# Other constants, and a shared port, in the model that orders TensorE's work in a two-layer decoder trunk

## The chip, the core and the metric

The kernel runs on one core of a Trainium2 chip. A core has TensorE (PE: matrix multiplications into PSUM), VectorE (DVE), ScalarE (ACT), GpSimd (POOL) and SyncE (SP, which here only issues DMAs). Each engine works through its own queue in order, and semaphores make an instruction wait for one on another engine. The metric is the device time in microseconds; less is better.

## The reference

A sequence of 1024 tokens of width 1024 goes through two layers, in float32. The first layer has a combined projection that feeds sliding-window attention (8 query heads, 2 key heads, window 128, rotary positions, a learned sink per head) and four heads of a gated delta rule in chunks; both outputs are concatenated and projected. The second layer is a recurrent block: a gate branch, a causal convolution of width 4 and a linear recurrence over time. Behind each mixer, and behind each MLP, stands a layer norm of `alpha * x + y`:

```
for layer in range(DEPTH):
    mix = hybrid_mixer(x, ...) if layer % 2 == 0 else recurrent_mixer(x, ...)
    x = layer_norm(DN_ALPHA * x + mix, ln1_g[layer], ln1_b[layer])
    x = layer_norm(DN_ALPHA * x + sqrelu_mlp(x, mlp_w1[layer], mlp_w2[layer]), ln2_g[layer], ln2_b[layer])
```

The MLP is `relu(x @ w1) ** 2 @ w2` with 4096 hidden units.

## The kernel before

**Precision.** Large products are made of three fp32r matmuls: each operand is split into a high part (a cast to fp32r) and a low part (the rest), and `mm3` (line 359) adds high by high, high by low and low by high. Every block of weights (128 x 1024, tile `ws`) is therefore cast to `wh` on ScalarE, or every fifth one on VectorE, and subtracted into `wl` on VectorE, or in some stages every second one on GpSimd (`split` and `wblock`, lines 343 to 357). Activations are split in the same way. The small products inside attention and the delta rule are plain fp32 matmuls.

**Streams and mixers.** The sequence is cut in two halves of 512 tokens, and each half is a stream (`stream`, line 1332) that runs through hybrid layer, MLP, recurrent layer and MLP, as a Python generator that yields after every few matmuls. A second kind of generator, a mixer, holds a chain of small steps in which TensorE and the other engines take turns: attention of a block of 128 queries (`attn_prep`, `attn_block`), one head of the delta rule (`head_mid`, line 949), the transposes of a layer norm (`layernorm`, line 451). A mixer yields a function of time, as `at(...)` (line 219), before each step of TensorE that needs a result of another engine.

**The order.** The loop at line 1361 writes TensorE's order by hand. While tracing, an object of the class `Clock` (line 60) keeps a model of the engines: a list of placed operations for VectorE (V), ScalarE (S), GpSimd (G) and DMA (D), and `now`, the time at which TensorE would be free. If a mixer's step is ready 0.5 us before `now` (MARGIN, line 27), its TensorE instructions are emitted next, and otherwise a unit of a stream. Each TensorE instruction is tied to the one before it (`_pe`, line 196). So the model's times decide how many matmuls of the streams stand between two steps of a chain; a step that comes too early in that order makes TensorE wait, for everything behind it too.

In the model `issue` (line 141) takes the ends of the operations that wrote the inputs, adds a hop for the consuming engine (`HOP`), and `place` (line 114) finds the next free spot on the engine's list and pushes what stands behind it. A duration is a constant and a slope per element (`NS`). `ready` (line 111) adds TensorE's hop. A matmul is costed in `matmul` (line 203):

```
c = 0.00042 * n * (1 if rhs.dtype == F32R else 4) if lhsT.shape[-1] > 32 else 0.046
```

The model also picks which tile of a ring is used next (`touch`, line 77: the one last used longest ago) and when the DMAs of `w2_sums` (line 515) are issued, which add quarters of w2 in DRAM, one on SyncE's queue and one, accumulating, on GpSimd's. The order of VectorE, ScalarE and GpSimd is set elsewhere: a scheduler that sees the whole program orders them with costs of its own.

Of the kernel before, what the change touches and what calls it, by code (L numbers as in the profile page):

```python
# [10 lines left out]
F32R = mybir.dt.float32r  # L11
# [4 lines left out]
PSUM = bass.MemoryType.PSUM  # L16

P = 128
D = 1024
# [30 lines left out]
NOSYNC = mybir.DependencyInfo(mybir.DependencyClass.NoSync, mybir.DependencyReason.SCHED_ONLY)  # L50


class Op:
    __slots__ = ("key", "t", "c", "end", "lag", "users")

    def __init__(self, key, t, c, lag=0.0):
        self.key, self.t, self.c, self.end, self.lag, self.users = key, t, c, t + c + lag, lag, []


class Clock:  # L60

    HOP = dict(V=0.3, S=0.3, G=0.3, P=0.40, D=0.0)
    NS = dict(V=(0.07, 1.04e-3), S=(0.095, 0.83e-3), G=(0.073, 2.25e-3))

    def __init__(self, tc, nc):
        self.tc, self.pe, self.now, self.last = tc, nc.tensor, 0.0, None
# [47 lines left out]
    def place(self, op, t):  # L114
        q = self.queue[op.key]
        i = bisect.bisect_left(q, t, key=lambda x: x.t)
        if i and q[i - 1].t + q[i - 1].c > t:
            t = q[i - 1].t + q[i - 1].c
        while i < len(q) and q[i].t <= t:
            t = max(t, q[i].t + q[i].c)  # L120
            i += 1
        op.t, op.end = t, t + op.c + op.lag
        q.insert(i, op)
        e = t + op.c
        while i + 1 < len(q) and q[i + 1].t < e:
            self.push(q[i + 1], e)

    def push(self, op, t):
        if t > op.t and op in self.queue[op.key]:
            self.queue[op.key].remove(op)  # L130
            self.place(op, t)
            for u in op.users:
                self.push(u, op.end + self.HOP[u.key])

# [3 lines left out]
        for a in outs:  # L138
            self.written.setdefault(a.name, {})[self.span(a)] = op

    def issue(self, key, outs, ins, c, t=0.0, lag=0.0, fresh=True):
        src = list(self.hits((self.written,), ins))
        war = list(self.hits((self.read, self.written), outs)) if fresh else []
        t = max([t] + [o.end + self.HOP[key] for o in src] + [o.end for o in war])
        for a in outs:
            t = max(t, self.old.get(a.name, 0.0), self.first.get(self.tag.get(a.name), 0.0))
        op = Op(key, t, c, lag)
        if key != "P":
            q = self.queue[key]
            while len(q) > 600:  # L150
                q.pop(0)
            self.place(op, t)
            for o in src + war:
                o.users.append(op)
        for a in outs:
            if a.name in self.tag:
                self.first[self.tag.pop(a.name)] = self.old[a.name] = op.t
        self.note(op, outs, ins)
        if key == "P":
            self.held.add(outs[0].name)  # L160
        else:
            self.held.difference_update(a.name for a in ins)
        return op

    def engine(self, eng, key):
        clk = self

        class Engine:
            def __getattr__(self, op):
                f = getattr(eng, op)  # L170

                def call(*a, **k):
                    aps = [x for x in (*a, *k.values()) if isinstance(x, bass.AP)]
                    outs = aps[:1] + ([k["accum_out"]] if "accum_out" in k else [])
                    if op == "tensor_tensor_reduce":
                        outs.append(aps.pop())
                    ins = aps[1:]
                    r = f(*a, **k)  # L178
# [24 lines left out]
    def matmul(self, out, lhsT, rhs, start, stop, fresh=False):  # L203
        n = int(np.prod(rhs.shape[1:]))
        c = 0.00042 * n * (1 if rhs.dtype == F32R else 4) if lhsT.shape[-1] > 32 else 0.046
        ins = self.pe.matmul(out, lhsT, rhs, start=start, stop=stop, skip_group_check=fresh)  # L206
        return self._pe(ins, out, [lhsT, rhs], c, start or fresh)

    def transpose(self, out, x, ident):
        return self._pe(self.pe.transpose(out, x, ident), out, [x], 0.00042 * 2 * out.shape[-1])  # L210


@with_exitstack
# [1293 lines left out]
```

## Time and profile before

| | |
|---|---|
| Median of 3 runs | 2313.34 us (2312.12 to 2314.28) |
| Profiled execution | 2313.61 us, span of its instructions 2311.8 us |
| TensorE busy | 2226.8 us (96%), 12460 matmuls |
| VectorE busy | 1552.7 us (67%) |
| ScalarE busy | 1026.1 us (44%) |
| GpSimd busy | 313.6 us (14%) |
| Mean granted TensorE clock | 0.988 of full |

In the lines of the profile PE is TensorE's matmuls, PEld its weight loads, and L178 and L206 are the lines of the model's helpers through which nearly every instruction is issued, so groups are told apart by their tiles: `wh` and `wl` are split weights, `ws` weights as loaded, `g`, `t`, `s` and `f` rings of activations, `mm` and `mx` PSUM banks of streams and mixers, `asc` and `hsc` small scalars of attention and of the delta rule, `lnw` those of layer norms, `S` the state of the delta rule. `mx<-t` is an operation that reads `t` and writes `mx`. In a row of a group, "busy, mean ns | idle before" follow the count. In the timeline a row has its start, its duration, and in brackets how long its engine sat idle before it and what ended that. TensorE's busy time counts an operation to its modelled end, so short waits between pipelined matmuls do not show as idle.

### The profile page before, as it was taken

What the parts mean: (1) busy time and instruction counts of PE and PEld (TensorE: products, weight loads), DVE (VectorE), ACT (ScalarE), POOL (GpSimd) and SP (SyncE); (2) the same over time, 40 slices, a digit from 0 to 9 for tenths busy, and PEclk for the clock granted to TensorE, in tenths of its full rate; (3) what the DMA queues carried; (4) which work ended last, traced back from release to release, by engine and by line L of the source; (5) the groups of instructions that cost most, each with busy time, mean ns of one, the idle gap of its engine ahead of it and who ended that gap; (6) DMA issues with size and microseconds to landing.
All of it is one profiled execution on the core that took longest, in us unless ns stands there. A gap on an engine that the chain in (4) does not pass through costs nothing.

```text
span 2311.8 us, 32057 instructions
## 1 busy us (share of the span) xinstructions
PE 2226.8 (96%) x12460; PEld 1795.1 (78%) x12460; DVE 1552.7 (67%) x2706; ACT 1026.1 (44%) x1759; POOL 313.6 (14%) x248
## 2 busy tenths in 40 slices
PE   8999997999999999999999999989999999999997
PEld 7676776667777888788888878868888887888886
DVE  6788759456645463686666898675565566776477
ACT  5364424433433233454444677474424434444442
POOL 3433223223322120000000001021100000000100
PEclk9999998999999999999999999999999999999999
DMA  4221232556667656677744335222523443454341
GB/s 159 65 74 36 75 123 74 146 153 180 178 177 231 193 162 187 191 237 232 222 139 155 119 129 170 93 74 96 182 95 127 138 146 125 156 166 137 128 159 69
DMA packets 86200, 329.08 MB, mean 142 GB/s; under 512 B 9504, under 2 KB 9888, under 8 KB 77856
## 3 DMA queue, kind: packets, MB, share of 16 engines
q1 hardware_dynamic: 72944, 272.17, 34.4%
q0 software_dynamic: 4608, 33.56, 7.6%
q10 hardware_dynamic: 8496, 21.30, 2.7%
q8 instruction: 98, 1.61, 0.3%
q14 instruction: 54, 0.44, 0.1%
HBM read 318.60 MB, written 75.50 MB: 170 GB/s over the span
## 4 chain that ended last, share of the span: by engine, by line
PE 78%; DVE 13%; ACT 3%; issue 2%; POOL 0%; DMA 0%; DVEq 0%; ACTq 0%; POOLq 0%
PE mm L206 61%; PE mx L206 16%; DVE g L178 5%; DVE t L178 2%; DVE s L178 2%; DVE hsc L178 2%; DVE wl L178 1%; PE mx L210 1%; DVE f L178 1%; ACT wh L178 1%; ACT g L178 1%; ACT t L178 1%; ACT s L178 1%; ACT f L178 0%; ACT L178 0%
## 5 line engine op out<-in xcount | busy, mean ns | idle before, releaser
L206 PE MATMUL mm<-g,wh 128*128 128x512 f32 x2816 | 890.1, 397 | 2.7 <-DVE g L178 2.6
L178 DVE TENSOR_TENSOR wl<-ws,wh 128x1024 fp32r<-128x1024 f32 (+1 forms) x374 | 456.8, 1222 | 340.0 <-ACT wh L178 336.7
L178 ACT CAST wh<-ws 128x1024 fp32r<-128x1024 f32 (+1 forms) x350 | 365.1, 1043 | 719.9 <-PE mm L206 620.6
L206 PEld LDWEIGHTS mm<-g,wh 128*128 128x128 f32 x2816 | 522.2, 189 | 111.3 <-DVE g L178 3.9
L206 PE MATMUL mm<-g,wl 128*128 128x512 f32 x1408 | 551.8, 392 | 0.0
L206 PE MATMUL mm<-wh,s 128*128 128x512 f32 x1152 | 379.8, 395 | 3.6 <-DVE g L178 3.3
L206 PEld LDWEIGHTS mm<-g,wl 128*128 128x128 f32 x1408 | 266.0, 189 | 57.0
L178 POOL TENSOR_TENSOR wl<-ws,wh 128x1024 fp32r<-128x1024 f32 (+1 forms) x64 | 157.2, 2457 | 1010.1 <-ACT wh L178 861.4
L206 PEld LDWEIGHTS mm<-wh,s 128*128 128x128 f32 x1152 | 216.2, 188 | 51.1 <-DVE g L178 3.9
L206 PE MATMUL mm<-wh,g 128*128 128x512 f32 (+1 forms) x768 | 231.4, 379 | 9.3 <-ACT wh L178 6.4
L206 PE MATMUL mm<-wl,s 128*128 128x512 f32 x576 | 224.6, 390 | 0.0
L206 PE MATMUL mx<-wh,s 128*128 128x512 f32 x528 | 172.7, 392 | 1.8 <-DVE s L178 1.8
L206 PEld LDWEIGHTS mm<-wh,g 128*128 128x128 f32 x768 | 142.3, 190 | 35.9 <-ACT wh L178 6.4
L206 PE MATMUL mm<-wl,g 128*128 128x512 f32 (+1 forms) x384 | 143.8, 375 | 0.3 <-DVE wl L178 0.3
L178 ACT CAST s<-g 128x512 fp32r<-128x512 f32 x158 | 96.4, 623 | 100.3 <-PE mm L206 51.2
L178 DVE TENSOR_TENSOR s<-g,s 128x512 fp32r<-128x512 f32 x158 | 106.8, 687 | 38.7 <-ACT s L178 38.5
L206 PEld LDWEIGHTS mm<-wl,s 128*128 128x128 f32 x576 | 108.3, 188 | 20.6 <-DVE wl L178 0.3
L206 PEld LDWEIGHTS mx<-wh,s 128*128 128x128 f32 x528 | 99.1, 188 | 23.2 <-DVE s L178 3.1
L178 DVE CAST wh<-ws 128x1024 fp32r<-128x1024 f32 x88 | 62.7, 712 | 78.1 <-PE mm L206 68.4
L178 DVE TENSOR_TENSOR g<-g,mm 128x512 f32<-128x512 f32 x144 | 95.0, 683 | 20.0 <-PE mm L206 19.5
L206 PE MATMUL mx<-wl,s 128*128 128x512 f32 x264 | 102.8, 389 | 0.0
L206 PEld LDWEIGHTS mm<-wl,g 128*128 128x128 f32 x384 | 73.2, 191 | 12.2 <-DVE wl L178 0.6
(241 smaller groups left out, 2703.2 us busy)
## 6 DMA issues: line engine op xcount, KB each, us to landing
ws<-w SPq DMA_DIRECT2D x234, 512.0 KB, 3.3
ws<-t SPq DMA_DIRECT2D x88, 512.0 KB, 3.3
t<-w POOLq DMA_DIRECT2D x32, 1024.0 KB, 8.6
ws<-hin_fm SPq DMA_DIRECT2D x32, 512.0 KB, 3.3
t<-w SPq DMA_DIRECT2D x16, 1024.0 KB, 7.5
t<-t SPq DMA_DIRECT2D x16, 1024.0 KB, 6.5
ws<-rin SPq DMA_DIRECT2D x32, 512.0 KB, 3.3
ws<-hout SPq DMA_DIRECT2D x16, 512.0 KB, 3.3
```

The source lines that it names most:

```text
L178: r = f(*a, **k)
L206: ins = self.pe.matmul(out, lhsT, rhs, start=start, stop=stop, skip_group_check=fresh)
L210: return self._pe(self.pe.transpose(out, x, ident), out, [x], 0.00042 * 2 * out.shape[-1])
```

## The change

The edit lies in the model alone. The hop that a consumer adds shrinks (V and S 0.3 to 0.06, G 0.3 to 0.1, P 0.40 to 0.3), and each operation instead has a lag after its duration that also counts for whoever overwrites its operands (V 0.085, S 0.1, G 0.08, P 0.17). TensorE's `now` leaves the lag out, and a matmul no longer waits for an earlier matmul on the same bank. An fp32r matmul is costed at 0.443 ns a column instead of 0.42; an fp32 one at 0.04 us and 1.2 ns a column (2 ns where the output has 64 rows and n is over 128) instead of 1.68 ns a column; one with at most 32 output rows at 0.03 us instead of 0.046. A scan on VectorE has twice the slope, a `scalar_tensor_tensor` of 128 elements or more 0.05 us more. New is the port: all operations of G, and those of V named in `PORT` whose operands all lie in SBUF, exclude each other, both when an operation is placed (`shared`) and when one that is placed later pushes others back.

```
+PORT = {"tensor_tensor", "scalar_tensor_tensor", "tensor_scalar"}
...
-    HOP = dict(V=0.3, S=0.3, G=0.3, P=0.40, D=0.0)
-    NS = dict(V=(0.07, 1.04e-3), S=(0.095, 0.83e-3), G=(0.073, 2.25e-3))
+    HOP = dict(V=0.06, S=0.06, G=0.1, P=0.3, D=0.0)
+    NS = dict(V=(0.07, 1.04e-3), S=(0.1, 0.83e-3), G=(0.07, 2.27e-3))
+    LAG = dict(V=0.085, S=0.1, G=0.08, P=0.17)
...
+    def shared(self, key, t):
+        q = self.queue["G" if key == "V" else "V"]
+        i = bisect.bisect_right(q, t, key=lambda x: x.t)
+        return q[i - 1].t + q[i - 1].c if i and q[i - 1].port and q[i - 1].t + q[i - 1].c > t else t
+
+    def place(self, op, t):
+        q = self.queue[op.key]
+        while True:
+            i, t = self.gap(op.key, t)
+            u = self.shared(op.key, t) if op.port else t
+            if u <= t:
+                break
+            t = u
         op.t, op.end = t, t + op.c + op.lag
         q.insert(i, op)
         e = t + op.c
         while i + 1 < len(q) and q[i + 1].t < e:
             self.push(q[i + 1], e)
+        if op.port:
+            r = self.queue["G" if op.key == "V" else "V"]
+            for o in r[bisect.bisect_right(r, t, key=lambda x: x.t):][:20]:
+                if o.t >= e:
+                    break
+                if o.port:
+                    self.push(o, e)
...
-        war = list(self.hits((self.read, self.written), outs)) if fresh else []
+        war = [o for o in self.hits((self.read, self.written), outs) if key != "P" or o.key != "P"] if fresh else []
...
-                    if key == "V" and op == "tensor_copy" and ins[0].space != PSUM:
+                    sbuf = all(x.space != PSUM for x in ins + outs)
+                    if key == "V" and op == "tensor_copy" and sbuf:
                         c1 *= 0.5
-                    clk.issue(key, outs, ins, c0 + c1 * n)
+                    if op == "tensor_tensor_scan":
+                        c1 *= 2.0
+                    if op == "scalar_tensor_tensor" and n >= 128:
+                        c0 += 0.05
+                    port = key == "G" or (key == "V" and sbuf and op in PORT)
+                    clk.issue(key, outs, ins, c0 + c1 * n, 0.0, clk.LAG[key], True, port)
...
-        self.now = self.issue("P", [out], reads, cost, self.now, 0.0, fresh).end
+        o = self.issue("P", [out], reads, cost, self.now, self.LAG["P"], fresh)
+        self.now = o.t + o.c
...
-        c = 0.00042 * n * (1 if rhs.dtype == F32R else 4) if lhsT.shape[-1] > 32 else 0.046
+        if rhs.dtype == F32R:
+            c = 0.000443 * n
+        elif lhsT.shape[-1] <= 32:
+            c = 0.03
+        else:
+            c = 0.04 + (0.002 if n > 128 and lhsT.shape[-1] == 64 else 0.0012) * n
...
-        return self._pe(self.pe.transpose(out, x, ident), out, [x], 0.00042 * 2 * out.shape[-1])
+        return self._pe(self.pe.transpose(out, x, ident), out, [x], 0.00085 * out.shape[-1])
```

More of the change, by code (lines that the diff above doesn't have):

```diff
@@ L50, with __init__ @@
 NOSYNC = mybir.DependencyInfo(mybir.DependencyClass.NoSync, mybir.DependencyReason.SCHED_ONLY)
+PORT = {"tensor_tensor", "scalar_tensor_tensor", "tensor_scalar"}
 class Op:
-    __slots__ = ("key", "t", "c", "end", "lag", "users")
-    def __init__(self, key, t, c, lag=0.0):
+    __slots__ = ("key", "t", "c", "end", "lag", "users", "port")
+    def __init__(self, key, t, c, lag=0.0, port=False):
         self.key, self.t, self.c, self.end, self.lag, self.users = key, t, c, t + c + lag, lag, []
+        self.port = port
 class Clock:
-    HOP = dict(V=0.3, S=0.3, G=0.3, P=0.40, D=0.0)
-    NS = dict(V=(0.07, 1.04e-3), S=(0.095, 0.83e-3), G=(0.073, 2.25e-3))
+    HOP = dict(V=0.06, S=0.06, G=0.1, P=0.3, D=0.0)
+    NS = dict(V=(0.07, 1.04e-3), S=(0.1, 0.83e-3), G=(0.07, 2.27e-3))
+    LAG = dict(V=0.085, S=0.1, G=0.08, P=0.17)
     def __init__(self, tc, nc):
@@ L112, in ready, with gap @@
         return max((o.end for o in self.hits((self.written,), aps)), default=0.0) + self.HOP["P"]
-    def place(self, op, t):
-        q = self.queue[op.key]
+    def gap(self, key, t):
+        q = self.queue[key]
         i = bisect.bisect_left(q, t, key=lambda x: x.t)
@@ L121, in place @@
             i += 1
+        return i, t
+    def shared(self, key, t):
[10 more added lines that the diff above has]
+            t = u
         op.t, op.end = t, t + op.c + op.lag
@@ L139, in note, with issue @@
             self.written.setdefault(a.name, {})[self.span(a)] = op
-    def issue(self, key, outs, ins, c, t=0.0, lag=0.0, fresh=True):
+    def issue(self, key, outs, ins, c, t=0.0, lag=0.0, fresh=True, port=False):
         src = list(self.hits((self.written,), ins))
-        war = list(self.hits((self.read, self.written), outs)) if fresh else []
+        war = [o for o in self.hits((self.read, self.written), outs) if key != "P" or o.key != "P"] if fresh else []
         t = max([t] + [o.end + self.HOP[key] for o in src] + [o.end for o in war])
@@ L146, in issue @@
             t = max(t, self.old.get(a.name, 0.0), self.first.get(self.tag.get(a.name), 0.0))
-        op = Op(key, t, c, lag)
+        op = Op(key, t, c, lag, port)
         if key != "P":
```

## The prediction, made before the result was known

> **What bounds the kernel now.** I read the page's busy shares first, then one table of five stretches (core 0, busy time of PE, PEld, DVE, ACT, POOL in each, then the granted clock).
>
> ```profile
> span 2311.8 us, 32057 instructions
> PE 2226.8 (96%) x12460; PEld 1795.1 (78%) x12460; DVE 1552.7 (67%) x2706; ACT 1026.1 (44%) x1759; POOL 313.6 (14%) x248
> ...
> 17.00:751.40 734.40, 689.72 (x5608) 527.89 (x5607) 493.42 (x1161) 300.83 (x749) 220.82 (x172) 0.97 0.42 125
> 751.40:1502.80 751.40, 744.16 (x3333) 612.71 (x3332) 521.00 (x775) 361.81 (x510) 45.28 (x49) 1.00 0.54 171
> 1502.80:1530.00 27.20, 18.91 (x87) 14.70 (x86) 23.88 (x35) 21.59 (x34) 4.67 (x2) 0.81 0.18 59
> 1530.00:2254.20 724.20, 719.23 (x3182) 593.62 (x3181) 459.98 (x606) 320.09 (x437) 39.72 (x18) 1.00 0.41 136
> 2254.20:2311.80 57.60, 44.49 (x196) 36.18 (x194) 42.78 (x98) 12.79 (x17) 0.00 (x0) 0.92 0.19 68
> ```
>
> TensorE is the bound, and the change takes no work from it. Only its idle time can be won: 734.4 - 689.7 = 44.7 us in the first stretch (attention and delta rule between matmuls), 7.2, 8.3 and 5.0 in the next three. The last stretch's 13.1 is mostly the final layer norm, which nothing can fill. Then the stretches in which the granted clock is a half, up to 751 us and the one at 1510:
>
> ```profile
> 144.96:151.79 6.83, 6.02 (x20) 5.24 (x21) 5.77 (x25) 5.78 (x23) 0.74 (x1) 0.50 0.02 7
> 192.75:199.57 6.83, 6.05 (x46) 2.94 (x48) 5.68 (x14) 2.33 (x4) 1.28 (x1) 0.50 0.07 23
> 366.83:370.24 3.41, 3.41 (x11) 2.83 (x10) 3.41 (x10) 1.06 (x2) 0.00 (x0) 0.50 0.00 0
> 383.89:390.72 6.83, 3.03 (x38) 2.51 (x39) 6.83 (x16) 4.55 (x17) 1.60 (x3) 0.50 0.00 0
> 397.55:407.79 10.24, 8.21 (x51) 5.04 (x51) 7.14 (x14) 1.66 (x3) 4.29 (x3) 0.50 0.39 120
> 633.07:636.48 3.41, 3.41 (x26) 2.23 (x28) 1.31 (x2) 0.57 (x1) 0.00 (x0) 0.50 1.10 190
> 1510.29:1520.53 10.24, 5.77 (x14) 3.90 (x15) 9.63 (x15) 4.93 (x8) 4.02 (x2) 0.50 0.17 51
> ```
>
> The first six hold 30.1 us of PE work at half speed, so 15.1 us are lost there; the last loses 2.9. What a better order could win at most is 44.7 + 15.1 = 59.8 us in the first stretch, 8.3 + 2.9 = 11.2 around 1510, and 12.2 elsewhere. Whom PE waits for (total us, times, longest), from the view of waits:
>
> ```profile
> PE mx L206 <- DVE t L178: 16.3, 8, 7.0
> PE mx L210 <- DVE g L178: 15.2, 9, 5.7
> PE mm L206 <- DVE g L178: 9.6, 11, 2.2
> ...
> PE mx L206 <- DVE s L178: 6.3, 7, 2.6
> PE mx L206 <- DVE S L178: 5.3, 3, 3.0
> PE mx L206 <- DVE g L178: 3.9, 3, 2.2
> PE mx L206 <- ACT t L178: 3.2, 4, 1.2
> ```
>
> These 45 waits are for VectorE nearly always: a small group was put into TensorE's order before its operand was there. The longest, in the timeline (start, duration; POOL, then DVE, then PE):
>
> ```profile
> 375.43 1.34 POOL L178 TENSOR_TENSOR f<-f,t 128x512 f32<-128x512 f32 x1 [11.36 <-PE mx L210]
> 378.41 2.41 POOL L178 TENSOR_TENSOR wl<-ws,wh 128x1024 fp32r<-128x1024 f32 x1 [1.63 <-ACT wh L178]
> ...
> 375.65 5.71 DVE L178 TENSOR_TENSOR g<-g,s 128x512 f32<-128x512 f32 x4
> ...
> 381.89 1.15 DVE L178 SCALAR_TENSOR_TENSOR f<-f,sm,f 128x512 f32<-128x512 f32 x1
> ...
> 383.24 1.88 DVE L178 TENSOR_TENSOR g<-g,s 128x512 f32<-128x512 f32 x3
> ...
> 387.69 0.65 PE L206 MATMUL mx<-t 32*32 32x32 f32 x32 [7.00 <-DVE t L178]
> ```
>
> Three of those DVE operations take 1.88 us where nothing is beside them, four take 5.71 beside POOL: 5.71 - 4 x 0.63 = 3.2 us too long. The scalar_tensor_tensor's 1.15 also overlaps POOL work; against the 0.63 that is 0.5. So 3.7 of the 7.0 us are VectorE and GpSimd excluding each other. That this is general shows in the spread (min/median/max ns) of two groups of tiny or equal DVE operations:
>
> ```profile
> L178 DVE TENSOR_TENSOR g<-g,asc x24: 426/1174/2875, 122.9 to 499.4; 128x512 f32<-128x512 f32 x21, 128x256 f32<-128x256 f32 x3
> L178 DVE TENSOR_TENSOR hsc<-hsc x128: 149/164/2478, 45.9 to 780.1; 128x4 f32<-128x4 f32 x80, 128x8 f32<-128x8 f32 x48
> ```
>
> The longest of a four-element operation is 2.5 us, as long as one POOL split of weights (2.41 above).
>
> **The change, part by part.** No instruction is added or removed; places in TensorE's order move, and with them buffers (picked by the model's last use) and the program order of what feeds them. Its time is the same matmuls plus the idle above, so I price each part in idle.
>
> *Port.* The model now pushes a VectorE operation with all operands in SBUF behind a GpSimd one and the reverse, and what depends on it. A step that was issued too early then gets more matmuls ahead of it. By the 3.7 of 7.0 us I give the port half of the first stretch's loss: 29.9 us. How much is caught? None if the collisions fall elsewhere than in the model, 29.9 if all are foreseen. A split on POOL starts when ScalarE has cast its block, which the model times too, but VectorE's order is not written by this model. I take two thirds: -20 us. Around 1510 the wait began before POOL worked at all, so I take nothing there:
>
> ```profile
> 1505.88 0.60 PE L210 MATMUL mx<-csb,g 128*128 128x128 f32 x4
> ...
> 1509.64 4.08 POOL L178 TENSOR_TENSOR wl<-ws,wh 128x1024 fp32r<-128x1024 f32 x1 [18.84 <-DVE g L178]
> ...
> 1512.17 1.11 PE L210 MATMUL mx<-csb,g 128*128 128x128 f32 x4 [5.69 <-DVE g L178]
> ```
>
> *Rule on the same port.* In the first stretch 17 DVE casts of weights have a mean of 803 ns, while all 88 have 712:
>
> ```profile
> L178 DVE CAST wh<-ws 128x1024 fp32r<-128x1024 f32 (+1 forms) x17 | 13.7, 803 | 16.4 <-PE mm L206 16.4
> ...
> L178 DVE CAST wh<-ws 128x1024 fp32r<-128x1024 f32 x88 | 62.7, 712 | 78.1 <-PE mm L206 68.4
> ```
>
> The other 71 then have 690, so casts too are held up, by 17 x 113 ns = 1.9 us; the changed model leaves tensor_copy out of its set. The Trainium skill (SBUF — State Buffer, "Who interferes with whom") says the same against the change: copies and casts can take the shared pair as well, and whoever starts first keeps it for the whole instruction. By that the term would be some 2 us smaller; the trace agrees on the direction, with 1.9 us.
>
> *Shorter hops.* A PE-VectorE-PE step on 128x512 was counted 0.3 + 0.602 + 0.4 = 1.302 us and is now 0.23 + 0.687 + 0.3 = 1.217; every further link VectorE to VectorE loses 0.155, ScalarE to VectorE 0.14. A real fp32r matmul takes 226.7 ns (72 in 16.32), which the model counted 215 and now counts 226.8, so the same wait is covered by 5% fewer of them.
>
> ```profile
> 1039.60 16.32 PE mm L206 x72
> ```
>
> Both take cover away: about 0.2 us per step (0.1 to 0.35 by the number of links). If the 45 waits become 30, these lengthen by 6 us; if all 45 stay, by 16 at 0.35.
>
> *fp32 costs on TensorE.* These the model overstates, and time that it believes has passed is cover that a chain beside it does not have. Sixteen score matmuls take 1.10 us to the next start, 32 of the 32x32 kind 0.38:
>
> ```profile
> 370.86 1.16 PE L206 MATMUL mx<-kT,g 64*128 64x128 f32 x16
> 371.96 0.73 PE L206 MATMUL mm<-g,wh 128*128 128x512 f32 x2
> ...
> 391.65 0.45 PE L206 MATMUL mx<-t 32*32 32x32 f32 x32
> 392.03 0.73 PE L206 MATMUL mm<-g,wh 128*128 128x512 f32 x2
> ```
>
> Counted before 3.44 and 1.47, now 3.10 and 0.96. The excess shrinks from 2.34 to 2.00 and from 1.09 to 0.58: so the durations are not as the trace shows here, only nearer. I put -1 us (0 to -6) on it.
>
> *Scans twice as long, scalar_tensor_tensor 50 ns more, ScalarE's and GpSimd's constants.* Zero: they move a few readings by under 0.6 us in a stage whose filler matmuls (744.2 of 751.4 us busy) hide it; without that cover the 16 scans would cost 16 x 0.53 = 8.5.
>
> *What else moves.* The DMAs that add up quarters of w2 are released by the model's time, which runs nearer to real time, so they come about 5% earlier in the order, on SP's and POOL's queues. POOL already waits for the first half of such a sum before it issues the second, with splits of weights queued behind (us, times, longest):
>
> ```profile
> POOL t L178 <- DMA t<-t: 187.6, 8, 28.2
> ```
>
> PE never waits for a POOL split in the rows above, so zero; without that cover one split could be up to 28 us late.
>
> Sum against the profiled execution, 2313.6 us (span 2311.8 and 1.8 around it; 0.3 over the median of the runs): -20 + 6 - 1 = -15, so 2298.6, or **2298** as a median. Its own range: gain 29.9 + 6 with no loss gives 2277; catching a third (-10) with 6 of loss gives 2310.
>
> **Rivals.**
> *Caught whole.* If every collision is foreseen, the long waits go, and with them the half clock that follows each. 29.9 + the other half of the clock's 15.1 = 37.4: **2276**. For it: all six half-clock stretches up to 751 us lie on or behind a long wait. Against it: DVE's order. The Trainium skill (TensorE: Matmul & The Clock Gate, "What's actually happening") says the clock falls to half only after an idle window of about 3.4 us; the trace's 3.41, 6.83 and 10.24 us stretches agree. By that rule trimming the waits below a window would give back the whole 15.1 rather than a share.
>
> *Leaner cover, slower.* Mechanism: steps of delta rule and layer norm are issued 0.2 to 0.35 us earlier, VectorE's backlog is not seen, and PE waits at each. For it: the 5.7 us wait that ends at 1512 began without the port. Price: 45 x 0.35 = 16 us, and in the other stretches half of their 23.4 us again, 12; less 10 for a third of the port: +18, **2331**. It decides once the port brings less than the hops cost, that is if fewer than about a quarter of the collisions are placed right.
>
> *It does nothing.* VectorE, ScalarE and GpSimd follow an order that this model does not write; collisions then fall at random against it, and 7 us of gain meets 6 of loss: 2312.
>
> **How the numbers follow.** Forecast 0.48, caught whole 0.13, nothing 0.14, slower 0.25. A move under 0.2% (4.6 us) cannot be told from none here. Faster: 0.48 + 0.13, less a little of the forecast's upper end, 0.60; same 0.15; slower 0.25. The range takes in the whole catch and the slower case's middle: 2270 to 2332.
>
> **What would show it.** Right: in the first stretch PE's idle falls from 44.7 to about 30, half-clock stretches from six to three or four, and the 7.0 us wait is gone, while DVE's long operations (2.5 to 2.9 us) stay, since the change avoids no collision. Hops wrong if there are more than 45 waits for DVE, short ones, at L210 above all. The prediction is wrong if idle moves in the stretches after 751 us, or if the DVE operations themselves get longer.

## The result, and the profile after

The changed kernel took **2349.48 us** (median; 2347.53 to 2350.66) against 2313.3 us for the kernel before: a ratio of **1.0156, 95% interval 1.0138 to 1.0173**. It is slower by 36 us, on the other side of the forecast and above the end of the range.

The page of the changed kernel, its span and the share of each engine:

```profile
span 2345.8 us, 32052 instructions
PE 2234.1 (95%) x12436; PEld 1799.4 (77%) x12436; DVE 1561.7 (67%) x2729; ACT 1037.0 (44%) x1770; POOL 304.0 (13%) x240
```

The span grew by 34.0 us. TensorE's idle time, span less busy, went from 2311.8 - 2226.8 = 85.0 to 2345.8 - 2234.1 = 111.7, which is 26.7 of the 34.0. The other 7.3 is TensorE's busy time, although there are 24 records of matmuls fewer: more of them ran at half clock (mean granted clock 0.980, before 0.988). Where the idle time lies, in the table of stretches (columns as in the prediction: busy time of PE, PEld, DVE, ACT, POOL, then granted clock):

```profile
17.00:751.40 734.40, 674.63 (x5532) 516.52 (x5531) 486.28 (x1179) 298.81 (x752) 210.15 (x166) 0.96 0.38 115
751.40:1502.80 751.40, 733.89 (x3254) 602.33 (x3253) 514.32 (x716) 355.86 (x491) 48.37 (x46) 1.00 0.57 181
1502.80:2254.20 751.40, 736.39 (x3242) 605.78 (x3241) 483.01 (x676) 346.38 (x477) 42.45 (x21) 0.99 0.39 130
```

The first stretch has 734.40 - 674.63 = 59.8 us of idle instead of 44.7; the second 17.5 instead of 7.2; the third 15.0 instead of 8.3 + 5.0 = 13.3. Because the kernel is later all along, these are the same times and not quite the same work, but the sign is clear: 15 and 10 us of new idle, where the forecast had -15 in the first. The half-clock stretches of the first 751 us, in the same view:

```profile
102.80:106.20 3.40, 3.40 (x57) 2.30 (x48) 2.35 (x8) 0.25 (x1) 0.00 (x0) 0.51 0.62 189
143.80:150.60 6.80, 6.80 (x34) 4.66 (x34) 3.63 (x11) 1.29 (x4) 0.86 (x3) 0.50 0.00 0
212.10:218.90 6.80, 5.33 (x51) 4.24 (x50) 5.17 (x10) 1.67 (x6) 0.94 (x1) 0.50 0.14 40
270.10:273.50 3.40, 3.40 (x32) 2.95 (x19) 2.86 (x15) 0.74 (x2) 0.00 (x0) 0.50 0.47 163
341.80:362.30 20.50, 11.23 (x149) 6.64 (x150) 16.12 (x28) 7.25 (x18) 7.93 (x5) 0.50 0.08 30
444.20:468.10 23.90, 9.81 (x28) 5.15 (x29) 20.59 (x59) 11.00 (x27) 2.43 (x2) 0.50 0.43 110
```

There are six, as before, but they cover 64.8 us instead of 37.6, and two are longer than any before. Behind 751 us, and before the last layer norm, come three more of 6.8 us each, at 1052, 1530 and 1547, where the kernel before had one of 10.2. Whom TensorE waits for (total us, times, longest):

```profile
PE mx L250 <- DVE g L206: 20.3, 15, 4.5
PE mx L246 <- DVE t L206: 19.3, 12, 7.1
PE mx L250 <- issue: 12.2, 2, 11.1
PE mx L246 <- DVE s L206: 6.9, 4, 3.5
...
PE mm L246 <- DVE g L206: 6.4, 9, 2.4
PE mx L246 <- DVE g L206: 5.4, 2, 4.0
PE mm L246 <- DVE wl L206: 5.2, 3, 3.7
```

L246 and L250 are the L206 and L210 of before, and L206 here is the old L178. The two kinds that led before have grown (`t` from 16.3 to 19.3 us, `g` at the transposes from 15.2 to 20.3), while `mm` waits less for `g` (6.4, before 9.6). All waits for VectorE together went from 50 with 62.5 us to 54 with 75.6. New is one of 11.1 us which the profile gives to no single releaser ("issue"), and waits for `wl`, a weight split on VectorE, went from 0.3 us to 5.2. Both are read below, under the prediction's steps.

### The profile page after: what moved, and what is told of

Read it like the earlier page. It is cut to its first block, busy times and chain, and to the rows that moved or that the text cites. A ratio compares the mean times of both kernels' runs of the same rounds, so it can differ in the third digit from the quotient of the medians.

```text
span 2345.8 us, 32052 instructions
## 1 busy us (share of the span) xinstructions
PE 2234.1 (95%) x12436; PEld 1799.4 (77%) x12436; DVE 1561.7 (67%) x2729; ACT 1037.0 (44%) x1770; POOL 304.0 (13%) x240
## 4 chain that ended last, share of the span: by engine, by line
PE 52%; DVE 5%; ACT 2%; issue 1%; DMA 0%; DVEq 0%; ACTq 0%
PE mm L246 41%; PE mx L246 11%; DVE g L206 2%; DVE wl L206 1%; DVE s L206 1%; ACT wh L206 0%; DVE t L206 0%; PE mx L250 0%; ACT s L206 0%; ACT t L206 0%; ACT g L206 0%; ACT L206 0%; ACT f L206 0%; DVE lnw L206 0%; DMA ws<-w 0%
## 5 line engine op out<-in xcount | busy, mean ns | idle before, releaser
L246 PE MATMUL mm<-g,wh 128*128 128x512 f32 x2816 | 884.1, 395 | 3.2 <-DVE g L206 2.8
L206 DVE TENSOR_TENSOR wl<-ws,wh 128x1024 fp32r<-128x1024 f32 (+1 forms) x388 | 473.1, 1220 | 367.2 <-ACT wh L206 363.1
L206 ACT CAST wh<-ws 128x1024 fp32r<-128x1024 f32 (+1 forms) x356 | 371.4, 1043 | 686.0 <-PE mm L246 594.3
L246 PEld LDWEIGHTS mm<-g,wh 128*128 128x128 f32 x2816 | 523.5, 189 | 114.8 <-DVE g L206 4.6
L246 PE MATMUL mm<-g,wl 128*128 128x512 f32 x1408 | 550.4, 391 | 3.7 <-DVE wl L206 3.7
L246 PE MATMUL mm<-wh,s 128*128 128x512 f32 x1088 | 356.9, 394 | 3.8 <-DVE g L206 3.6
L246 PEld LDWEIGHTS mm<-g,wl 128*128 128x128 f32 x1408 | 265.2, 188 | 60.4 <-DVE wl L206 4.2
L206 POOL TENSOR_TENSOR wl<-ws,wh 128x1024 fp32r<-128x1024 f32 (+1 forms) x56 | 132.5, 2366 | 918.8 <-DVE wh L206 583.3
L246 PE MATMUL mm<-wh,g 128*128 128x512 f32 (+1 forms) x768 | 241.5, 385 | 6.5 <-ACT wh L206 6.5
L246 PEld LDWEIGHTS mm<-wh,s 128*128 128x128 f32 x1088 | 204.4, 188 | 48.5 <-DVE g L206 5.3
L246 PE MATMUL mm<-wl,s 128*128 128x512 f32 x544 | 212.0, 390 | 1.3 <-DVE wl L206 1.3
L246 PE MATMUL mx<-wh,s 128*128 128x512 f32 x576 | 189.2, 392 | 0.0
L246 PEld LDWEIGHTS mm<-wh,g 128*128 128x128 f32 x768 | 143.2, 191 | 32.8 <-ACT wh L206 6.5
L206 ACT CAST s<-g 128x512 fp32r<-128x512 f32 x172 | 105.0, 623 | 103.9 <-PE mm L246 58.2
L206 DVE TENSOR_TENSOR s<-g,s 128x512 fp32r<-128x512 f32 x172 | 116.0, 685 | 45.4 <-ACT s L206 45.4
L246 PE MATMUL mm<-wl,g 128*128 128x512 f32 (+1 forms) x384 | 144.6, 376 | 0.2 <-DVE wl L206 0.2
L246 PEld LDWEIGHTS mx<-wh,s 128*128 128x128 f32 x576 | 108.2, 188 | 21.8
L246 PEld LDWEIGHTS mm<-wl,s 128*128 128x128 f32 x544 | 102.2, 188 | 21.2 <-DVE wl L206 1.7
L246 PE MATMUL mx<-wl,s 128*128 128x512 f32 x288 | 112.0, 389 | 0.0
L206 DVE CAST wh<-ws 128x1024 fp32r<-128x1024 f32 x88 | 60.6, 689 | 65.6 <-PE mm L246 60.8
L206 DVE TENSOR_TENSOR g<-g,mm 128x512 f32<-128x512 f32 x136 | 89.6, 682 | 12.3 <-PE mm L246 11.8
L206 ACT ACTIVATE g<-mm 128x512 f32<-128x512 f32 x100 | 59.3, 593 | 79.6 <-PE mm L246 76.1
```

## The experiments

Beside every run the kernel before ran on the same chip and took 2311.9 to 2313.3 us; ratios are to that. "Draw" in this text is one order among the many that small edits give.

| Run | Edit | us | Ratio, 95% interval |
|---|---|---|---|
| e1_hops_only | before, new HOP and LAG alone | 2334.30 | 1.0090 (1.0061 to 1.0119) |
| e2_pe_only | before, new costs of TensorE alone | 2337.28 | 1.0103 (1.0072 to 1.0134) |
| e3_port_only | before, the port alone | 2331.46 | 1.0078 (1.0049 to 1.0107) |
| e4_old_hops | after, old HOP, no LAG | 2340.85 | 1.0118 (1.0089 to 1.0148) |
| e5_before_margin52 | before, MARGIN 0.52 | 2325.82 | 1.0054 (1.0031 to 1.0077) |
| e13_before_margin48 | before, MARGIN 0.48 | 2321.44 | 1.0038 (1.0026 to 1.0050) |
| e6_before_cost421 | before, matmuls at 0.000421 us a column, not 0.00042 | 2342.77 | 1.0127 (1.0098 to 1.0156) |
| e7_after_margin52 | after, MARGIN 0.52 | 2331.63 | 1.0078 (1.0055 to 1.0101) |
| e14_after_margin48 | after, MARGIN 0.48 | 2349.58 | 1.0156 (1.0126 to 1.0185) |
| e8_after_margin100 | after, MARGIN 1.0 | 2356.68 | 1.0187 (1.0158 to 1.0217) |
| e9_after_pull | after, engines drawn to the model's order | 2368.87 | 1.0242 (1.0212 to 1.0271) |
| e10_before_pull | before, the same edges | 2342.84 | 1.0129 (1.0100 to 1.0159) |
| e11_before_no_pool_splits | before, no split on GpSimd | 2302.99 | 0.9960 (0.9940 to 0.9979) |
| e12_after_no_pool_splits | after, no split on GpSimd | 2330.70 | 1.0075 (1.0051 to 1.0098) |
| e15_before_no_pool_margin52 | e5 with no split on GpSimd | 2313.78 | 1.0005 (0.9993 to 1.0016) |
| e16_before_no_pool_arithmetic | before, no tensor_tensor on GpSimd | 2294.12 | 0.9916 (0.9887 to 0.9945) |
| e17_after_six_straight | after, six plain blocks in the first MLP | 2360.13 | 1.0206 (1.0176 to 1.0235) |
| e18_before_four_straight | before, four of them | 2317.08 | 1.0020 (1.0008 to 1.0031) |

### The parts by themselves

First theory (1 in the expectations): the model issues steps too early now (thin cover). Against it stood the other parts of the change. With all parts taken back, the changed code writes the order of before on every engine, so the parts are the whole of the change.

e1 takes over only HOP and LAG, e2 only the costs of TensorE, e3 only the port; e4 is the changed kernel with HOP and LAG undone. (All four have the rule that a matmul does not wait for an earlier one on its bank; without LAG it changes nothing.) ("before" in minus, "after" in plus.)

```diff
-    HOP = dict(V=0.3, S=0.3, G=0.3, P=0.40, D=0.0)
+    HOP = dict(V=0.06, S=0.06, G=0.1, P=0.3, D=0.0)
+    LAG = dict(V=0.085, S=0.1, G=0.08, P=0.17)
...
-        c = 0.00042 * n * (1 if rhs.dtype == F32R else 4) if lhsT.shape[-1] > 32 else 0.046
+        if rhs.dtype == F32R:
+            c = 0.000443 * n
+        elif lhsT.shape[-1] <= 32:
+            c = 0.03
...
+                    port = key == "G" or (key == "V" and sbuf and op in PORT)
```

> The kernel before with the new hops and lags alone; matmul costs, port and VectorE's extra durations stay as before. Theory 1 (the thinner allowance for hops makes TensorE's small steps come too early): slower by most of the 36 us, 2335 to 2350 us, and about 20 more waits of PE for DVE than before. Theory 2 (the costs of matmuls do it): 2310 to 2318. Theory 3 (the port misplaces VectorE's work in the model): 2310 to 2318. Theory 4 (any change of these constants draws another order, and orders scatter): anywhere from 2300 to 2350, with no relation to the other parts' sum.

> The kernel before with the new costs of matmuls and transposes alone. Theory 1: 2308 to 2320, since an fp32r matmul now counts 5% more and thins the cover by about 0.1 us a step only. Theory 2: 2335 to 2350. Theory 3: 2308 to 2320. Theory 4: anywhere from 2300 to 2350.

> The kernel before with the shared port alone (and VectorE's longer scans and the small changes of ScalarE's and GpSimd's durations); hops and matmul costs as before. Theory 1: 2290 to 2310, faster, as the port alone only adds cover. Theory 2: the same. Theory 3: 2335 to 2350. Theory 4: anywhere from 2300 to 2350.

The kernel of e3 has the port alone; the longer scans and the small durations that this text names with it were not in it.

> The changed kernel with the old hops (0.3 us, 0.40 for TensorE) and no lags; all else as changed. Theory 1: the loss is gone, 2290 to 2315 us, and the waits of PE for DVE fall to the 45 of before or fewer. Theory 2 and theory 3: the loss stays, 2340 to 2350. Theory 4: anywhere from 2300 to 2350.

Measured: 2334.3, 2337.3 and 2331.5 for each part alone, and 2340.9 with all parts but the hops. Each part alone costs 18 to 24 us, together 63, where the whole costs 36. e4 misses what thin cover had named (2290 to 2315), and no theory of a single guilty part had all three parts slower. Parts that are so alike, and whose sum is nearly twice the whole, made me ask whether any other order would cost as much.

The port alone, which the prediction prices at -20, shows where the time can go. Its page, and its first stretch:

```profile
span 2331.1 us, 32055 instructions
PE 2244.2 (96%) x12460; PEld 1810.2 (78%) x12460; DVE 1535.1 (66%) x2706; ACT 1030.4 (44%) x1759; POOL 311.7 (13%) x248
...
17.00:751.40 734.40, 689.38 (x5566) 530.31 (x5565) 475.92 (x1164) 301.96 (x751) 215.04 (x169) 0.96 0.39 117
```

TensorE's idle time is 86.9 us, where before had 85.0, and in the first stretch 45.0, where before had 44.7. Nearly all of the 19 us by which the span is longer is TensorE's busy time, 17.4 us more for the same 12460 records, at a mean granted clock of 0.981 instead of 0.988.

### Edits without a meaning

MARGIN moves by 4%, or the cost of a matmul by 0.24%: no theory of the engines says that these matter. MARGIN 1.0, on the other hand, doubles the margin, and should help if cover was what lacked.

```diff
-MARGIN = 0.5
+MARGIN = 0.52
```

(0.48 in e13 and e14, 1.0 in e8; in e6 instead:)

```diff
-        c = 0.00042 * n * (1 if rhs.dtype == F32R else 4) if lhsT.shape[-1] > 32 else 0.046
+        c = 0.000421 * n * (1 if rhs.dtype == F32R else 4) if lhsT.shape[-1] > 32 else 0.046
```

> The kernel before with the margin ahead of a mixer's step at 0.52 us instead of 0.50, and nothing else: a change with no meaning in itself, that only draws another order. Theory 4 in its strong form (the order of the kernel before is a lucky draw, and any other draw costs about what each part cost): 2325 to 2345 us. Against it (each part of the change does harm of its own): 2308 to 2318.

> The kernel before with 0.421 ns a column for an fp32r matmul in the model instead of 0.420, and nothing else: again a change without meaning. Lucky draw: 2325 to 2345 us. Harm of each part's own: 2308 to 2318.

> The changed kernel with the margin at 0.52 us. Lucky draw: the changed kernel is one draw too, so this lies within 15 us of 2349 on either side, most likely under it, 2330 to 2350. Harm of the change's own: 2345 to 2352.

> The changed kernel with the margin at 1.00 us, which gives every step 0.5 us of cover back, more than the shorter hops took. Theory 1 (thin cover): 2300 to 2320 us, with fewer than 45 waits of PE for DVE of any length. Lucky draw: 2320 to 2350, no better than the other draws.

> The kernel before with the margin at 0.48 us: a further draw without meaning. Luck of the draw: 2322 to 2345, slower than the kernel before once more. If the order of the kernel before is not special: 2308 to 2318.

> The changed kernel with the margin at 0.48 us. Luck of the draw alone (the two models draw from the same spread, 2325 to 2350): anywhere in it. The change harms beyond the draw: over 2345.

The kernel before moved by +12.5, +29.5 and +8.1 us; the changed one by -17.9 and +0.1. An order written from the model's times is a draw: a step that falls on the other side of the margin moves everything behind it. In the stretches of e6, the dearest of the three, the idle lies in the second stretch (751.40 - 730.24 = 21.2 us, before 7.2), though the edit knows no stretch:

```profile
17.00:751.40 734.40, 686.48 (x5629) 527.17 (x5628) 500.82 (x1190) 302.87 (x758) 218.69 (x170) 0.98 0.40 121
751.40:1502.80 751.40, 730.24 (x3202) 599.11 (x3201) 513.35 (x720) 356.44 (x492) 36.05 (x42) 0.98 0.56 176
```

With double the margin the changed kernel took 2356.7, above either range named for it, so thin cover by itself falls as the cause.

### Drawing the other engines to the model's order

The model's list was laid beside VectorE's queue, instruction by instruction. Of the 2664 pairs of neighbours in the queue 646 stand the other way round in the model's list, 488 of them by more than 1 us (before: 633 and 458 of 2641). A theory then (5) was that the model would be right if the engines did what it assumed. These runs add order edges without a wait, from each instruction of V, S and G to the one before it on the model's list:

```diff
-                    clk.issue(key, outs, ins, c0 + c1 * n, 0.0, clk.LAG[key], True, port)
+                    clk.made.append((clk.issue(key, outs, ins, c0 + c1 * n, 0.0, clk.LAG[key], True, port), r))
...
+    for key in "VSG":
+        made, seen = [x for x in clk.made if x[0].key == key], []
+        for o, r in made:
+            i = bisect.bisect_right(seen, o.t, key=lambda x: x[0].t)
+            if i:
+                tc.add_manual_dep(r.ins, seen[i - 1][1].ins.name, NOSYNC, reason="as modelled")
+            seen.insert(i, (o, r))
```

> The changed kernel, with an ordering edge (no wait, only order) on VectorE, ScalarE and GpSimd from each operation to the one that was emitted earlier and stands nearest before it in the model's list; the pairs of neighbours in VectorE's queue that stand more than 1 us the wrong way round in the model's list fall from 488 to 309 of 2664. Theory 5 (the durations are right, but VectorE's queue is not in the model's order, so what the model foresees happens elsewhere): clearly faster than every draw of the changed kernel so far, under 2325 us, and PE's idle in the first 750 us under 50 us. Theory 4 alone (luck of the draw): 2325 to 2355.

> The same edges in the kernel before (458 pairs to 268 of 2641). Theory 5: the old model profits less, since its durations are off: 2315 to 2335, slower than the changed kernel with these edges. Theory 4 alone: another draw, 2320 to 2345.

The pairs that stand the wrong way by more than 1 us fell from 488 to 309 and from 458 to 268, and the kernels took 2368.9 and 2342.8: 19 and 30 us more. Both are slower, e9 beyond either range named for it. In the stretches of e9 the first has 734.40 - 667.06 = 67.3 us of idle and the second 23.3, the most of all runs:

```profile
17.00:751.40 734.40, 667.06 (x5487) 510.36 (x5486) 486.84 (x1177) 296.35 (x750) 209.60 (x165) 0.96 0.37 113
751.40:1502.80 751.40, 728.10 (x3217) 597.43 (x3216) 510.50 (x707) 354.44 (x491) 38.86 (x47) 0.99 0.58 181
```

So an order nearer to the model's was not faster. But the edges do not reach far: 309 pairs stay wrong, and of the 83 VectorE instructions that GpSimd holds up in e9 the model foresees 22, hardly a larger share than without the edges (21 of 90, counted below). What a model would give whose order holds was therefore not tested.

### Taking the collisions away

If VectorE and GpSimd exclude each other, removing GpSimd's work removes the cost, whatever the order. e11, e12 and e15 put all weight splits on VectorE:

```diff
-        (G if key else V).tensor_tensor(l, x, h, ALU.subtract)
+        V.tensor_tensor(l, x, h, ALU.subtract)
```

e16 does it with each of GpSimd's tensor_tensor (eight lines in all), of which for example

```diff
-        G.tensor_tensor(av, xv, cs, ALU.mult)
+        V.tensor_tensor(av, xv, cs, ALU.mult)
...
-        G.tensor_tensor(v4(E), bc_mid(U, 4), bc_last(g, P), ALU.mult)
+        V.tensor_tensor(v4(E), bc_mid(U, 4), bc_last(g, P), ALU.mult)
```

GpSimd keeps narrow copies, memsets and DMAs.

> The kernel before, with all splits of weights subtracted on VectorE and none on GpSimd, so most of the shared port's collisions go while VectorE gets about 60 operations of 1.13 us more. Port as the main cause of PE's waits: the time that VectorE's operations last too long falls from about 105 to under 40 us, PE's idle and half-clock loss up to 751 us fall from about 60 to 40 us, 2290 to 2312 us. Luck of the draw and VectorE's load as the cause: 2320 to 2350 with no less idle.

> The changed kernel with no splits of weights on GpSimd. Port as the main cause, and foreseen wrongly: 2300 to 2325 us, 25 us or more under the changed kernel. Luck of the draw: 2325 to 2355.

> No splits of weights on GpSimd, in the kernel before with the margin at 0.52 us: a second draw of that. If taking the collisions away gains by itself: under the draw with the same margin and the splits on GpSimd (2326), 2295 to 2318. If 2303 was a lucky draw: 2320 to 2340.

> The kernel before with every elementwise operation of two operands on VectorE; GpSimd keeps copies of three columns, memsets and its DMAs. Collisions as the cause: VectorE's operations that last too long all but vanish (under 10 us), 2290 to 2310 us. VectorE's load takes over (some 70 operations of 0.6 us more): 2310 to 2335 us.

Without the splits: -10 us on before, -12 on before at MARGIN 0.52 (e15 to e5), -19 on after; without any GpSimd arithmetic -19, to **2294.1 us, the fastest of all kernels here**. Any one of these could be a lucky order, since e11 alone differs from before by no more than an edit without a meaning did, and e12 lies in the range named for luck (2325 to 2355) and not in that for the port (2300 to 2325). But four of four go the same way, and the trace shows that the collisions go. Count an instruction of VectorE as held up if it took over 0.1 us longer than the median of its form: before had 95, 105.5 us too long in all, every one beside a GpSimd instruction; e11 has 48 us left, more than the 40 it was expected to stay under; e16 none. The page of e16, then the same two groups as in the prediction, then its first stretch:

```profile
span 2293.2 us, 32016 instructions
...
PE 2214.8 (97%) x12436; PEld 1790.4 (78%) x12436; DVE 1574.7 (69%) x2865; ACT 1036.0 (45%) x1770; POOL 62.2 (3%) x104
...
L178 DVE TENSOR_TENSOR g<-g,asc x32: 418/684/693, 123.0 to 419.0; 128x512 f32<-128x512 f32 x28, 128x256 f32<-128x256 f32 x4
L178 DVE TENSOR_TENSOR hsc<-hsc x128: 118/160/169, 43.5 to 703.2; 128x4 f32<-128x4 f32 x80, 128x8 f32<-128x8 f32 x48
...
17.00:751.40 734.40, 700.75 (x5713) 543.18 (x5712) 510.15 (x1315) 306.68 (x761) 27.14 (x53) 0.98 0.42 126
```

The longest four-element operation takes 0.169 us where it took 2.478, and the 128 x 512 product 0.693 where it took 2.875. VectorE has 159 instructions more and is busy for only 22 us more, since it no longer stands still inside them. The first stretch's idle is 734.40 - 700.75 = 33.7 us, before 44.7; over the whole span it is 78.4 instead of 85.0. The other 12.0 of the 18.6 us are TensorE's busy time, and some 5.4 of them are 24 matmuls fewer, not collisions (24 x 226.7 ns, an estimate; the next section has the reason).

### The first MLP's form

One more rival (6): the changed model lets the first half's first MLP leave its plain form after four blocks instead of six, and that, not the places of the small steps, might make the difference. (The seven-product form then uses 24 matmuls fewer. e16 goes over after four as well.) e17 holds the changed kernel at six (first diff), e18 brings before to four (second).

```diff
-        while e < 8 and not ((c == 1 or sts[1].get("op", -1) >= layer) and rings["g"] >= 2 and e % 2 == 0):
+        pin = 6 if (layer, c) == (0, 0) else 0
+        while e < 8 and (e < pin or not ((c == 1 or sts[1].get("op", -1) >= layer) and rings["g"] >= 2 and e % 2 == 0)):
```

```diff
-        while e < 8 and not ((c == 1 or sts[1].get("op", -1) >= layer) and rings["g"] >= 2 and e % 2 == 0):
+        while e < 8 and (layer, c, e) != (0, 0, 4) and not ((c == 1 or sts[1].get("op", -1) >= layer) and rings["g"] >= 2 and e % 2 == 0):
```

> The changed kernel, with the MLP of the first layer's first half held to six plain blocks (as the kernel before has it by its model's times) before it goes over to products of the seven-product form; the changed model goes over after four. All draws that go over after four have been 2332 to 2350 us (mean 2342), those after six 2313 to 2334 (mean 2325), leaving kernels with other work on GpSimd aside. Theory 6 (the switch, taken earlier, costs some 17 us; the rest is draw): 2325 to 2340 us, the waits of 3.8 us for wl behind it gone. Draw alone: 2332 to 2350.

> The kernel before, made to go over after four plain blocks instead of six. Theory 6: 2322 to 2340 us, with a wait of PE of about 3.8 us for wl and idle of 10 us more around the first layer's second norm. The switch costs nothing: 2305 to 2318, as it saves 24 matmuls (5.4 us).

Undone in after it costs 11 us more instead of winning any, beyond both ranges named for it; done in before it costs 4, within what was named for a switch that costs nothing. The rival falls: it is one more draw on either side.

### What the draws say together

Take only edits in which the quality of a model has no part. Before and its four neighbours (e5, e6, e13, e18) have 2313.3, 2325.8, 2342.8, 2321.4 and 2317.1: mean 2324, standard deviation 11. After and its three (e7, e14, e17) have 2349.5, 2331.6, 2349.6 and 2360.1: mean 2348, standard deviation 12. The means are 24 us apart, about three standard errors (11.5 / sqrt 5 and 11.8 / sqrt 4 give 7.8 together); without before itself, which is the lowest of its five, 21. So of the 36 us **some 21 to 24 go with the changed model, give or take 8, and 11 to 14 are the good place of before's own order among its neighbours**, which any edit was likely to lose. Against the neighbours' mean of 2327 the single parts cost 7.5, 10.5 and 4.7 us; each lies within one draw's spread, so which part makes the 21 us stays open. The stretches give no more than a hint: the first one's idle is 58.7 us in e1, near the 59.8 of the changed kernel, and 42.7 in e2 and 45.0 in e3, but e7, with all parts in, has 46.8. More draws of each part would tell; they were not run.

## Why the prediction was wrong

**What bounds the kernel: right, but not as a yardstick.** TensorE is the bound, its work did not change, and the loss is idle and half clock. But the sum was made from before's own idle, as if that were what its model gives. It is the lowest of its five draws in time; its first stretch's 44.7 us of idle compare with 44.6 to 52.5 in the four neighbours. "I price each part in idle" left out the term which every such edit has, the new draw: +11 to +14 us on average here, give or take 11.

**Port: "I take two thirds: -20 us". This is the step that failed.** The part alone (e3) took 18 us more instead of 20 less, 4.7 over the neighbours' mean, and left the first stretch's idle where it was (45.0 us). The collisions are real, but taking them away won 10 to 19 us (e11, e12, e15, e16), less than the 29.9 that foreseeing them all was to win. And most were not foreseen. In the changed kernel's trace 90 VectorE instructions are held up, 88.9 us in all; its model sets 58 behind a GpSimd operation of over 0.3 us; 21 are the same ones. (With GpSimd's shorter ones counted it sets 77, of which 27 are the same.) That is 23 to 30% of the 90, about the quarter at which the prediction itself saw the port bring no more than the hops cost, where its sum had two thirds. The reason was in its own sentence, "VectorE's order is not written by this model": 488 neighbouring pairs are off by more than 1 us, and one split lasts 2.4 us. The sum had a second gap: it gave a collision foreseen where none happens no cost at all, and these are 37 of the 58 here. What they cost no run shows apart. And as foreseen, the change does not take the collisions away (88.9 us, before 105.5). The two groups in the changed kernel:

```profile
L206 DVE TENSOR_TENSOR g<-g,asc x24: 409/886/1752, 123.2 to 450.1; 128x512 f32<-128x512 f32 x21, 128x256 f32<-128x256 f32 x3
...
L206 DVE TENSOR_TENSOR hsc<-hsc x128: 149/164/2133, 46.0 to 731.0; 128x4 f32<-128x4 f32 x80, 128x8 f32<-128x8 f32 x48
```

**Rule on the same port.** The casts that the change leaves out of its set were the correction of 1.9 us. In the changed kernel none is held up (87 at a mean of 691 ns, the unhindered 690 of the prediction), so it was worth nothing here:

```profile
L206 DVE CAST wh<-ws 128x1024 fp32r<-128x1024 f32 x87 | 60.2, 691 | 65.2 <-PE mm L246 60.5 <-PE mx L246 4.5
```

The Trainium skill (SBUF — State Buffer, "Who interferes with whom") says that VectorE with two SBUF inputs contends with a GpSimd instruction that reads SBUF, and that who comes first holds the shared pair throughout. The runs agree: no operation more than 0.1 us over its form's median is left once GpSimd's arithmetic is gone (e16).

**Hops, +6.** The named sign came, at L250: 15 waits for `g` with a mean of 1.35 us, where L210 had 9 with 1.69. ("More than 45 waits for DVE" was no sign: the 45 are the seven rows shown, four of them for ScalarE, and before has 50 for VectorE in all.) Their size does not follow: the hops alone cost 7.5 us over the neighbours' mean, undoing them in the changed kernel gave 8.6 us (2349.5 to 2340.9), and either is inside one draw. The rival "leaner cover", nearest in time with 2331, is not thereby right: at twice the margin the kernel is no faster (e8).

**fp32 costs, -1.** Here rows were misread. The profile shows two records for each plain fp32 matmul that is no transpose: the program has eight matmuls in a score group, which stands as x16. The counted costs should have been half of what the prediction states, 1.72 and 0.74 us before, 1.55 and 0.48 now, against 1.10 and 0.38 measured. So the excess went from 0.62 and 0.36 to 0.45 and 0.10, not from 2.34 and 1.09 to 2.00 and 0.58: "only nearer" holds, its sizes do not. It moved the sum by 1 us, and the part alone was slower all the same (2337.3).

**What was costed at nothing.** "No instruction is added or removed" was wrong: the changed kernel has 24 records of TensorE fewer and 23 instructions of VectorE more, because the model's times also decide when the first MLP changes its form (e17 and e18: within the spread of the draws). Constants and scans were not run alone. The hiding work for splits did fail, though on VectorE and not on GpSimd: TensorE waited 5.2 us for `wl`. In the rows below the first of two splits is done only when TensorE starts, and TensorE has stood for 3.73 us; TensorE's order has no gate on a stream's weights, as it has `at` for a mixer's steps:

```profile
1051.66 2.34 DVE L206 TENSOR_TENSOR wl<-ws,wh 128x1024 fp32r<-128x1024 f32 x2
...
1052.92 0.80 PE L246 MATMUL mm<-g,wl 128*128 128x512 f32 x1 [3.73 <-DVE wl L206]
```

**The sign "the 7.0 us wait gone".** A wait of 7.1 us before the same kind of 32 x 32 matmuls is there, at 350 us, and the 11.1 us one is new. In the timeline around it (start, duration; PE, then DVE) the last matmul ends, and the transposes of a layer norm stand next in TensorE's order:

```profile
441.53 0.39 PE L246 MATMUL mm<-wh,g 128*128 128x512 f32 x1
453.01 1.09 PE L250 MATMUL mx<-csb,g 128*128 128x128 f32 x4 [11.10 <-issue]
```

```profile
441.96 0.75 DVE L206 SCALAR_TENSOR_TENSOR g<-g,lnw,s 128x512 f32<-128x512 f32 x1
...
444.50 1.20 DVE L206 TENSOR_TENSOR wl<-ws,wh 128x1024 fp32r<-128x1024 f32 x1
...
448.06 2.74 DVE L206 TENSOR_TENSOR g<-g,asc 128x512 f32<-128x512 f32 x3
...
452.17 0.74 DVE L206 SCALAR_TENSOR_TENSOR g<-g,lnw,s 128x512 f32<-128x512 f32 x1
```

VectorE works without a pause over these 11 us, through residual adds, statistics, a split, three products of attention and the norm's tiny steps, and only then comes to the norm's own output. The transposes start 0.10 us after its end; that they waited for it is inferred, since the profile names no releaser. The three products at 2.74 us are 0.9 above the 1.88 that three such take alone (the prediction's row), so the port has about 1 us in it; the rest is backlog in an order that the model does not know. The prediction saw this at 1512 ("the wait began before POOL worked at all") and took nothing for it; this is what a foreseen port could not mend. The other signs of being right failed as well: the first stretch's idle rose to 59.8 us instead of falling to about 30, and there are six half-clock stretches, not three or four. Its own sign of being wrong came: idle moved after 751 us, by 10 us in the second stretch.

**"Trimming the waits below a window".** The rival "caught whole" and the port's share of the clock loss took the clock to fall only behind a window of 3.4 us that is idle. The stretches' lengths fit such windows, but the windows just before them, in the kernel before, are not idle:

```profile
141.55:144.96 3.41, 1.20 (x6) 0.66 (x4) 3.31 (x10) 0.00 (x0) 2.04 (x2) 1.00 0.43 148
189.34:192.75 3.41, 1.61 (x38) 0.99 (x36) 3.38 (x4) 2.14 (x15) 3.35 (x3) 1.00 0.30 79
```

TensorE is busy for 1.20 and 1.61 of the 3.41 us, and the clock falls. Counted window by window over the traces of all twenty kernels (without their first 17 and last 60 us), it fell 209 times, only 23 of them behind a window idle throughout, and never behind one with less than 1.44 us of idle; it stayed full behind some with up to 1.88, and came back only behind windows with at most 0.60. So several short waits can do what a long one does. In e3 the longest wait for `t` is 1.2 us, where before had 7.0 (waits for `g` reach 6.4), and the clock was lower all the same.

**Chances.** Slower had 0.25, by a mechanism that the runs do not bear out, and the measured time lies above the range's end of 2332. A rival of this kind, "any other order is some 11 us worse, because this one is good", had neither a price nor a chance. Its price could not be read from one trace, but the direction could have been asked: is the order at hand a usual one for its model?

## What to carry to other kernels

An order written from a model's times is one draw among many: here edits that mean nothing moved the kernel before by 4 to 30 us and the changed one by 0 to 18, so judge a model by several draws of each version, and count the loss of a good draw into any change that touches the order. Try removing a contention before modelling it: modelled alone it came with 18 us more, taken away (144 instructions moved to the busier engine) with 19 less, though each is a single draw. A model that knows durations but not the order in which an engine takes its work placed few single collisions here, 21 of 90.

## What the hardware showed that was not expected

Small causes, long stretches: while it worked in pieces between waits, TensorE stayed at half clock for 20.5 and 23.9 us, busy 55% and 41% of them, where before no stretch was over 10.2. The Trainium skill (TensorE: Matmul & The Clock Gate, "What's actually happening") gives a window of about 3.4 us that must be busy before the clock rises; 3.4, 6.8, 20.5 and 23.9 are one, two, six and seven of them. A busy window did not always suffice, and the runs do not show why: from 143.80 to 150.60 TensorE is busy for all 6.80 us, with small matmuls, and stays at half clock for both windows. In the two long stretches the waits are paid for twice: 23.4 us of idle, and 10.5 us (an estimate, half of 11.23 + 9.81) for work at half speed. Such a stretch does not tell a slow kernel by itself, since e16, the fastest, has one of 23.9 us too.

GpSimd's 56 to 64 splits, at 2.4 us each, looked like help for VectorE; taking all of its tensor_tensor work off GpSimd raised VectorE's busy time by only 22 us of 1553, and the kernel gained 19.
